# An encoder's MLP on one Trainium2 core: up-projection by seven block products, down-projection as a stage of its own

## The chip, the cores and the metric

The kernel runs on 1 core of one Trainium2 chip. Its time is the device time of that core in microseconds (us). Before the change the median of three runs is 2946.79 us (2944.85 to 2953.02).

The engines have their own instruction queues and run side by side: PE (TensorE, matrix products), DVE (VectorE), ACT (ScalarE), POOL (GpSimd) and SP (SyncE, which issues all DMAs here). SBUF is the on-chip memory of 128 partitions, PSUM the eight banks of 128 x 512 fp32 into which PE writes and adds up, DRAM the memory outside. "128x512" is partitions x elements of a tile.

## The reference, cut to what matters

Two layers (an attention mixer each, A and B) run over 1152 tokens: 1024 of a prompt and 8 samples of 16. What the change touches is the MLP that ends each layer, D = 1024, D_FF = 2816:

```python
def conv_ffn(h, prev, w_up, conv_w, conv_b, w_down):
    u = h @ w_up                                   # (1152, 1024) @ (1024, 5632)
    ue = concatenate([prev, u], axis=1)            # prev: zeros, or the sample's state
    y = conv_b
    for tap in range(3):
        y = y + conv_w[tap] * ue[:, tap:tap + T]   # causal, over positions
    a, g = jnp.split(y, 2, axis=-1)
    out = (jax.nn.gelu(g) * a) @ w_down            # (1152, 2816) @ (2816, 1024)
    return out, ue[:, T:]                          # the last rows are an output too

h = x * (1 + sc_f) + sh_f
f, conv_rows = conv_ffn(h, ...)
x = layer_norm(ALPHA * x + (1 + g_f) * f, ln_g, ln_b)
```

All is fp32. After layer 0 the K and V of layer 1 are projected from its output.

## The kernel before, in words

**Products in three passes.** PE works on fp32r. Each operand is held as a high part (a cast) and a low part (the operand minus its high part), made by `split` (L157 the cast, on ACT as a rule, L168 the subtraction, on POOL for weights, on DVE for activations). A product is low x high + high x low + high x high, three matmuls that add up in one PSUM bank. H, the input of a projection, stands in SBUF as `H[128, 2, 8, 1152]`: two parts, eight blocks of 128 rows of D, 1152 tokens.

**Order.** The program is written in Python as one sequence; a scheduler places the instructions on the engines' queues by a time estimate of its own, in keeping with all dependencies. On the chip every queue runs in order, and an instruction that waits holds what stands behind it.

**Stages.** `opening`, `attention(0)`, `out_proj(0)`, `ffn(0)`, `attention(1)` (which begins with the projections of K and V), `out_proj(1)`, `ffn(1)`. `out_proj` works token tile by token tile (128 tokens, in the order 8, 0, 1, ..., 7) and closes each with `norm_tail`: the residual, layer norm, transposes on PE, the affine of the next stage, and the split into H. It shares the buffers of `ln_region` in the SBUF tile `F`.

**ffn.** D_FF is cut into 22 pieces j of 128 columns, each with an `a` half (gg = 0) and a `g` half (gg = 1) of the up weights. `up(j, gg)` loads one weight block of 128 x 1024 (512 KB, `wload`: a ring of two load buffers `ws`, then the split into a ring of four slots `wh`/`wl`) and runs three blocks of 384 to 388 tokens (`up_block`; `mmT`, L287): 24 matmuls into one bank. A block reaches back two to four tokens, so that the convolution can be done from PSUM at once (`conv`): one ACT pass (L1011) and two to four DVE taps (L1014) that read the bank, POOL's addition of the samples' state (L1029). For gg = 1 the GELU (L1058, ACT), the product with `a` (L1060, POOL) and a split into `X` follow. The gated activations of two j's thus stay in SBUF.

`down(g)` takes the two j's of group g: for each of nine token tiles and two halves of 512 output columns six matmuls (L1085) into a bank, which DVE adds to `acc[128, 9216]` in SBUF (L1076). Up blocks and down blocks of neighbouring groups interleave on PE. The last group (`down_last`) goes tile by tile, with the residual and the gate already in `acc` (`pregate`: L1144 on POOL, L1145 on DVE) and the gate in the weights; each tile is closed by `norm_tail` (layer 0) or `norm_last` (layer 1).

**Background.** In layer 0's ffn the adaLN projections of later stages (`ada`, L206 the loads, L214 the matmuls; 64 loads of 512 KB) run as background work, a bit per `wload`. At its start stand `tables_b` and `skew(1)`, which write the bias table of mixer B to DRAM: the copy L1187, 6144 KB.

Of the kernel before, what the change touches and what calls it, by code (L numbers as in the profile page):

```python
# [16 lines left out]
NT = 9  # L17
# [77 lines left out]
class Trunk:  # L95
    def __init__(self, ctx, tc, I, O):
# [9 lines left out]
        self.x2p = ctx.enter_context(tc.tile_pool(name="x2p", bufs=1))  # L106
# [8 lines left out]
        self.X2 = mem.tile([128, 3840], F32R, name="X2")  # L115
# [25 lines left out]
        self.hmD = dr.tile([NT, 128, 1024], F32, name="hmD")  # L141
        self.gd = dr.tile([4, 9, D], F32, name="gd")
# [192 lines left out]
    def vproj(self, l, q, banks, tmp):  # L335
# [4 lines left out]
        for t in LV:  # L340
# [20 lines left out]
    def attention(self, l, wk):  # L361
# [5 lines left out]
        self.X1 = self.x1p.tile([128, 9216], F32R, name=f"x1att{l}", tag="x1")  # L367
# [15 lines left out]
        x2b = self.x2p.tile([128, 768], F32, name=f"x2att{l}", tag="x2b")  # L383
        rb = x2b[:, 0:512]
        sd = Arena(x2b, 512)
# [14 lines left out]
        L = sd.take(128)  # L400
        M = sa.take(128) if l == 0 else None
        ost = sa.ring(1, 512) if l == 0 else sd.ring(2, 64)
# [485 lines left out]
    def norm_tail(self, t, x, xdst, aff, save, tb, eh, er, xrr, hfr, el="v", va=()):  # L888
# [5 lines left out]
        if aff is not None:  # L894
# [51 lines left out]
    def out_proj(self, l, xsrc, xdst, aff):  # L946
# [13 lines left out]
        tb = Ring([4, 5, 6, 7])  # L960
        for t in (8, 0, 1, 2, 3, 4, 5, 6, 7):
# [13 lines left out]
            self.norm_tail(t, x, xdst, aff, False, tb, "a", "pv", Ring([self.xr]), Ring([self.hf]))  # L975


    def ffn(self, l, xsrc, xdst, affs):
        nc, I, O, H = self.nc, self.I, self.O, self.H
# [3 lines left out]
        acc = self.x1p.tile([128, 9216], F32, name=f"acc{l}", tag="x1")  # L983
        if l == 0:
            self.tables_b(acc)
            self.skew(1)
        st = acc[:, 0:704]
        nc.sync.dma_start(st, I["sc"][l])
        s4 = st.rearrange("p (c s q) -> p c s q", c=44, s=8)
        t1 = acc[:, 704 : 704 + 352].rearrange("p (c s) -> p c s", s=8)  # L990
# [9 lines left out]

        ub = Ring([0, 1, 2])
        db = Ring([3, 4, 5])
        tb = Ring([6, 7])
        x2 = Arena(self.X2)
        x2b = self.x2p.tile([128, 768], F32R, name=f"x2ffn{l}", tag="x2b")
        aring = Ring([(x2.take(384), x2.take(384)) for _ in range(5)] + [(x2b[:, 0:384], x2b[:, 384:768])])

        def conv(ps, cc, bi, y):
            w = lambda i: cw[:, cc, i : i + 1]
            off = 0 if bi == 0 else 4  # L1010
            nc.scalar.activation(y, ps[:, off : off + 384], AF.Identity, bias=w(3), scale=w(2))  # L1011

            def tap(o, u, i):
                nc.vector.scalar_tensor_tensor(o, u, w(i), o, op0=ALU.mult, op1=ALU.add)  # L1014

            if bi == 0:
                tap(y[:, 1:384], ps[:, 0:383], 1)
                tap(y[:, 2:384], ps[:, 0:382], 0)
            elif bi == 1:
                tap(y, ps[:, 3:387], 1)  # L1020
                tap(y, ps[:, 2:386], 0)
            else:
                tap(y[:, 0:256], ps[:, 3:259], 1)
                tap(y[:, 0:256], ps[:, 2:258], 0)
                ys = y[:, 256:384].rearrange("p (s q) -> p s q", q=16)
                us = ps[:, 260:388].rearrange("p (s q) -> p s q", q=16)
                tap(ys[:, :, 1:16], us[:, :, 0:15], 1)
                tap(ys[:, :, 2:16], us[:, :, 0:14], 0)
                nc.gpsimd.tensor_add(ys[:, :, 0:2], ys[:, :, 0:2], E4[:, cc])  # L1029

        UB = ((0, 384), (380, 388), (764, 388))

        acts = {}
        ya = {}

        def up(j, gg):
            w = self.wload(I["wup"][l, j + 22 * gg])
            for bi in range(3):
                up_block(w, j, gg, bi)

        def up_block(w, j, gg, bi):
            cc = j + 22 * gg
            s0, n = UB[bi]
            ps = self.bank(ub.next())
            self.mmT(w, ps, s0, n)
            if gg == 0:
                y = ya[bi] = self.ya.next()
            else:
                y = self.yg.next()
            conv(ps, cc, bi, y)  # L1050
            if bi == 2:
                uo = self.uo[gg].rearrange("p (j s r) -> p j s r", s=9, r=2)
                src = ps[:, 258:402].rearrange("p (s q) -> p s q", q=16)[:, :, 0:2]
                nc.scalar.copy(uo[:, j % 11], src)
                if j % 11 == 10:
                    nc.sync.dma_start(O["conv"][l, gg, j // 11], self.uo[gg])
            if gg == 1:
                nc.scalar.activation(y, y, AF.Gelu_apprx_tanh)  # L1058
                a = self.at.next()
                nc.gpsimd.tensor_mul(a, y, ya[bi])  # L1060
                h, lo = aring.next()
                self.split(a, h, lo, "a", "v")
                acts[(j, bi)] = (h, lo)

        def down(g):
            js = (2 * g, 2 * g + 1)
            w = [self.wload(I["wdn"][l, j]) for j in js]
# [379 lines left out]
```

## Time and profile before

| | |
|---|---|
| runs | 2944.85, 2946.79, 2953.02 us |
| profiled execution: span (the page gives its time as this) | 2951.8 us, granted clock 0.986 |
| PE busy | 2826.3 us, 96% |
| DVE busy | 1530.0 us, 52% |
| ACT busy | 1136.0 us, 38% |
| POOL busy | 893.7 us, 30% |
| DMA | 353.97 MB, mean 120 GB/s |
| ffn(0) | first up block at about 483 us, end among the K and V projections, about 1390 us |
| ffn(1) | first up block at 2091 us, last matmul at 2934.7 us |

A row of a group reads: line, engine, operation, output <- inputs, shapes, count | busy us, mean ns of one | idle us of the engine just before it, and who ended that idle time. A row of the timeline reads: start us, length us, engine, line, operation, tiles, count, and in brackets the idle time before it with its releaser. A row of the chain of waits has start, length and what it was. PEld is PE's loading of the stationary operand, which overlaps the matmuls.

### The profile page before, as it was taken

The numbers are of one execution on the slowest core, as the hardware profiler recorded it, in microseconds if no ns is written. First come the engines' busy times: TensorE is split into PE (matmuls) and PEld (weight loads), VectorE is DVE, ScalarE is ACT, GpSimd is POOL, SyncE is SP. The second block draws the span as 40 slices with busy tenths as digits, with TensorE's granted clock in tenths as the row PEclk, the third lists the DMA queues.
The fourth block names the chain that finished last, engine by engine and source line by source line (L and its number), as shares of the span: only waits on it lengthen the run. The fifth ranks groups of instructions, "written<-read, shape, count | busy, mean of one in ns | idle before, by whom it ended". The sixth has DMA issues, their size and how long they took to land.

```text
span 2951.8 us, 43469 instructions
## 1 busy us (share of the span) xinstructions
PE 2826.3 (96%) x16774; PEld 2534.2 (86%) x16774; DVE 1530.0 (52%) x3349; ACT 1136.0 (38%) x2352; POOL 893.7 (30%) x657
## 2 busy tenths in 40 slices
PE   7999899999999999998999999879999999999996
PEld 5888678898999988987998888758999999999995
DVE  4476776234444444469113677667624444444468
ACT  3476634322222222225435666642442222222224
POOL 2122524232232222254641111321432222222253
PEclk9999899999999999999999999999999999999999
DMA  8655455423222222124875457763311111111121
GB/s 295 203 174 154 140 158 184 140 89 100 90 85 76 88 81 100 54 79 152 292 244 173 133 149 203 188 189 117 126 50 37 43 44 46 39 41 43 37 84 76
DMA packets 177839, 353.97 MB, mean 120 GB/s; under 512 B 34816, under 2 KB 93904, under 8 KB 177632
## 3 DMA queue, kind: packets, MB, share of 16 engines
q1 hardware_dynamic: 177632, 351.19, 37.3%
q8 instruction: 132, 2.16, 0.3%
q14 instruction: 75, 0.61, 0.1%
HBM read 285.22 MB, written 75.35 MB: 122 GB/s over the span
## 4 chain that ended last, share of the span: by engine, by line
PE 79%; DMA 7%; DVE 5%; POOL 3%; ACT 2%; issue 2%; SPq 1%; DVEq 0%; POOLq 0%; ACTq 0%
PE PS L287 43%; PE PS L1085 16%; PE PS L299 9%; PE PS L584 2%; PE PS L562 2%; PE PS L214 2%; PE PS L534 1%; DMA F<-in_adaw_dram 1%; PE PS L537 1%; POOL wl L168 1%; DMA ws<-oN 1%; PE PS L703 1%; DMA F<-zd 1%; PE PS L902 1%; DVE acc L1145 1%
## 5 line engine op out<-in xcount | busy, mean ns | idle before, releaser
L287 PE MATMUL PS<-H,wh 128*128 128x388 f32 (+1 forms) x5376 | 1024.0, 338 | 0.0
L287 PEld LDWEIGHTS PS<-H,wh 128*128 128x128 f32 x5376 | 948.2, 188 | 10.4 <-issue 1.9
L1014 DVE SCALAR_TENSOR_TENSOR F<-PS,F 128x256 f32<-128x256 f32 (+2 forms) x704 | 352.8, 512 | 525.0 <-ACT F L1011 511.8
L168 POOL TENSOR_TENSOR wl<-ws,wh 128x1024 fp32r<-128x1024 f32 x166 | 404.5, 2442 | 725.6 <-ACT wh L157 711.3
L287 PE MATMUL PS<-H,wl 128*128 128x384 f32 (+1 forms) x2688 | 550.0, 342 | 10.9 <-POOL wl L168 9.4
L287 PEld LDWEIGHTS PS<-H,wl 128*128 128x128 f32 x2688 | 477.0, 188 | 33.8 <-POOL wl L168 12.9
L1011 ACT ACTIVATE F<-PS,F 128x384 f32<-128x384 f32 x264 | 177.5, 672 | 746.9 <-PE PS L287 745.7
L1085 PE MATMUL PS<-wh,X 128*128 128x512 f32 x1320 | 412.1, 394 | 10.3 <-DVE acc L1076 4.2
L1076 DVE TENSOR_TENSOR acc<-acc,PS 128x512 f32<-128x512 f32 x324 | 221.4, 686 | 262.8 <-PE PS L1085 262.2
L1060 POOL TENSOR_TENSOR F<-F 128x384 f32<-128x384 f32 x132 | 138.3, 1048 | 639.7 <-ACT F L1058 638.4
L1085 PEld LDWEIGHTS PS<-wh,X 128*128 128x128 f32 x1320 | 245.3, 188 | 62.9 <-issue 6.2
L157 ACT CAST wh<-ws 128x1024 fp32r<-128x1024 f32 x174 | 180.0, 1045 | 152.8 <-PE PS L1085 74.7
L1085 PE MATMUL PS<-wl,X 128*128 128x512 f32 x660 | 216.2, 392 | 0.0
L299 PE MATMUL PS<-wh,H 128*128 128x256 f32 (+1 forms) x936 | 173.3, 314 | 7.6 <-DVE H L168 4.1
L299 PEld LDWEIGHTS PS<-wh,H 128*128 128x128 f32 x936 | 136.7, 194 | 18.0 <-DVE H L168 4.7
L168 DVE TENSOR_TENSOR X<-F,X 128x384 fp32r<-128x384 f32 x110 | 101.0, 918 | 92.3 <-ACT X L157 91.9
L1085 PEld LDWEIGHTS PS<-wl,X 128*128 128x128 f32 x660 | 124.1, 188 | 28.0
L562 PE MATMUL PS<-C,F 128*128 128x128 f32 x720 | 115.0, 285 | 23.9 <-DVE wh L569 12.2
L622 POOL TENSOR_TENSOR F<-F,x2att 64x512 f32<-64x512 f32 x62 | 79.4, 1281 | 191.0 <-DVE F L598 159.3
L299 PE MATMUL PS<-x1att,H 128*128 128x512 f32 x504 | 130.1, 399 | 4.2 <-ACT x1att L157 3.1
L562 PEld LDWEIGHTS PS<-C,F 128*128 128x128 f32 x720 | 85.6, 145 | 42.5 <-DVE wh L569 15.1
L1058 ACT ACTIVATE F<-F 128x384 f32<-128x384 f32 x132 | 69.2, 524 | 135.6 <-DVE F L1014 127.4
(220 smaller groups left out, 3479.4 us busy)
## 6 DMA issues: line engine op xcount, KB each, us to landing
ws<-in_wup_dram SPq DMA_DIRECT2D x88, 512.0 KB
F<-in_adaw_dram SPq DMA_DIRECT2D x80, 512.0 KB
ws<-in_wdn_dram SPq DMA_DIRECT2D x44, 512.0 KB
ws<-in_adaw_dram SPq DMA_DIRECT2D x32, 512.0 KB
x1att<-kH SPq DMA_DIRECT2D x60, 256.0 KB
xd<-F SPq DMA_DIRECT2D x27, 512.0 KB
F<-xd SPq DMA_DIRECT2D x27, 512.0 KB
vH<-X SPq DMA_DIRECT2D x40, 256.0 KB
```

Source lines behind the costliest of these rows:

```text
L157: nc.scalar.copy(out, in_)
L168: self.eng(el).tensor_sub(lo, src, hi.bitcast(F32))
L287: self.nc.tensor.matmul(out[:, 0:n], w[a][:, k * 128 : k * 128 + 128], H[:, p, k, s0 : s0 + n], start=i == 0, stop=i == 23)
L299: self.nc.tensor.matmul(out[:, 0:n], H[:, p, j * kn + k, t0 : t0 + 128], w[a][:, k * n : k * n + n], start=i == 0, stop=i == 23,)
L562: nc.tensor.transpose(t[:, n * 128 : n * 128 + 128], p[:, (kt - k0) * 128 : (kt - k0) * 128 + 128], self.ident)
L622: self.eng("v" if last else "p").tensor_mul(on[r, q], on[r, q], rb[r, :])
L1011: nc.scalar.activation(y, ps[:, off : off + 384], AF.Identity, bias=w(3), scale=w(2))
L1014: nc.vector.scalar_tensor_tensor(o, u, w(i), o, op0=ALU.mult, op1=ALU.add)
L1058: nc.scalar.activation(y, y, AF.Gelu_apprx_tanh)
L1060: nc.gpsimd.tensor_mul(a, y, ya[bi])
L1076: nc.vector.tensor_add(row[:, n], row[:, n], ps)
L1085: nc.tensor.matmul(ps, ac[m][p][:, cs], w[m][q][:, n], start=i == 0, stop=i == 5)
```

## The change

The up-projection of 42 of the 44 pieces goes over to Strassen's scheme (in Winograd's form). The product for one j is seen as 2 x 2 blocks. The weights (both halves of one j, `a` and `g`, by the two halves of D) give a11, a12, a21, a22; H by the two halves of D and by the two 64-token halves of each token tile gives b11, b12, b21, b22. Seven block products replace eight:

- The weights' combinations S1 to S3 and a21' are made per j by POOL (four operations of 128x512), and each of the seven sub-weights is split (ACT cast, DVE subtraction).
- H's combinations T1 to T4 are made once per layer (`combine`, `first`): `out_proj` stores the affine output of each tile to DRAM (`hD`), `combine` loads it tile by tile through two buffers, POOL and DVE combine, ACT and DVE split. T1 takes the place of b12 in H, T2 and T3 stand in the tile that was `acc`, T4 in X2.
- A product is 12 matmuls on 320 columns (token tiles 0 to 4) and 12 on 256 (tiles 5 to 8). Products that share terms add up in the same banks; ACT copies and DVE additions read the partial sums out into rows `ua`, `ug` of SBUF (`evict`).
- The convolution reads these rows (`conv_row`): passes of 1152 on ACT, taps of 1024 on DVE, all from SBUF. GELU and product follow on the whole row, and the gated row goes to DRAM (`actD`).
- The first j of each layer (NPL = 1) is computed as before (`plain`), while the combinations are made.
- The ring of load buffers has four entries in this stage; the ada loads of layer 0 go through it as well.

The down-projection is a stage of its own (`down`). Three groups of three token tiles are computed one after the other, each over all 22 j's, in six banks: nothing is added up in SBUF any more. Per group and j the weights are loaded and split again, and 128x384 of the gated activations are read back and split. The gate, the residual and the norm follow per tile (`tail`). In layer 1's last group six j's are held back and run tile by tile (KEEP). `tables_b`, `skew(1)` and the loads of gates and norm rows stand at the start of `down`. The diff, cut to its core:

```diff
-LO = ((0, 1, 2, 8, 3, 4, 5, 6, 7), (0, 1, 2, 3, 4, 5, 8, 6, 7))
-UP = ({0: (0, 1), 2: (2,)}, {0: (0, 1), 3: (2,)})
-LV = (0, 1, 2, 8, 3, 4, 5, 6, 7)
+LV = ((0, 1, 2, 8, 3, 4, 5, 6, 7), (0, 1, 2, 6, 7, 8, 3, 4, 5))
+GR = ((0, 1, 2), (6, 7, 8), (3, 4, 5))
+NPL = 1
+BGU = 0.5
+KEEP = 6
...
+        self.hD = dr.tile([NT, 128, 1024], F32, name="hD")
+        self.actD = dr.tile([NFF, 128, TOK], F32, name="actD")
...
+            if hdst is not None:
+                nc.sync.dma_start(hdst[t].rearrange("p (c t) -> p c t", t=128), h3)
...
+        def gated(j, ya, yg):
+            nc.scalar.activation(yg, yg, AF.Gelu_apprx_tanh)
+            nc.gpsimd.tensor_mul(yg, yg, ya)
+            nc.sync.dma_start(self.actD[j], yg)
...
+        def combine():
+            ring = Ring([F[:, 1536:2560], F[:, 7548:8572]])
+            for t in (8, 0, 1, 2, 3, 4, 5, 6, 7):
+                s = ring.next()
+                nc.sync.dma_start(s, self.hD[t])
...
+                x1 = T1S[:, :, t, :]
+                nc.gpsimd.tensor_sub(x1, b12, b11)
+                nc.gpsimd.tensor_sub(b12, b22, b12)
+                nc.vector.tensor_sub(b22, b22, x1)
+                nc.vector.tensor_sub(b21, b21, b22)
+                c = slice(64 * t, 64 * t + 64)
+                for src, (hi, lo) in ((b22, T2), (b12, T3), (b21, T4)):
+                    self.split(src, hi[:, :, c], lo[:, :, c], "a", "v")
...
+        def spair(j):
+            sa, sg = self.ws.next(), self.ws.next()
+            nc.sync.dma_start(sa, I["wup"][l, j])
+            nc.sync.dma_start(sg, I["wup"][l, j + 22])
+            a11, a12, a21, a22 = sa[:, 0:512], sa[:, 512:1024], sg[:, 0:512], sg[:, 512:1024]
+            E = nc.gpsimd
+            E.tensor_add(S1, a21, a22)
+            E.tensor_sub(S2, S1, a11)
+            E.tensor_sub(S3, a11, a21)
+            E.tensor_sub(a21, a12, S2)
...
+            plan = (
+                (a11, 11, 0, True),
+                (S2, 2, 1, True),
+                (a12, 21, 0, False),
+                (S3, 3, 1, False),
+                (S1, 1, 2, True),
+                (a22, 4, 1, False),
+                (a21, 22, 2, False),
+            )
+            for i, (src, q, g, start) in enumerate(plan):
+                w = sub.next()
+                self.split(src, *w, "a", "v")
+                x = operand(q)
+                for n in range(2):
...
+                    for a, p in ((1, 0), (0, 1), (0, 0)):
+                        for k in range(4):
+                            nc.tensor.matmul(
...
+                    evict(i, ps, n)
+                self.step(BGU)
+                if i == 5:
+                    yg = ys.next()
+                    conv_row(ug, j, 1, yg)
+            ya = ys.next()
+            conv_row(ua, j, 0, ya)
+            gated(j, ya, yg)
+
+        for j in range(NPL):
+            plain(j)
+        self.ws = wide
+        if l == 0:
+            self.bg = [self.ada(g, 7, wide) for g in (3, 4, 5, 6)]
+        combine()
+        first()
+        for j in range(NPL, NFF):
+            spair(j)
+        self.drain()
+        self.ws = narrow
+        self.down(l, xsrc, xdst, affs)
...
+        def fetch(j, t0):
+            w = self.wload(I["wdn"][l, j])
+            s = raw.next()
+            nc.sync.dma_start(s, self.actD[j][:, t0 * 128 : t0 * 128 + 384])
+            a = acts.next()
+            self.split(s, *a, "a", "v")
+            return w, a
...
+        for gi, g in enumerate(GR):
+            keep = KEEP if l and gi == 2 else 0
+            for j in range(NFF - keep):
+                w, a = fetch(j, g[0])
+                for i in range(3):
+                    mm(j, w, a, i)
+            if gi == 0:
+                aff = affs()
+            kept = [(j, *fetch(j, g[0])) for j in range(NFF - keep, NFF)]
+            for i, t in enumerate(g):
+                for j, w, a in kept:
+                    mm(j, w, a, i)
+                tail(t, i)
```

More of the change, by code (lines that the diff above doesn't have):

```diff
@@ L999, in ffn @@
         g.tensor_mul(E4[:, :, :, 1], s4[:, :, :, 1], wb(0))
-        ub = Ring([0, 1, 2])
[L1002 to L1009, printed above, removed]
+        ys = Ring([F[:, o : o + 1152] for o in (10492, 6396, 7548)])
@@ L1041, in up_block @@
-        def up_block(w, j, gg, bi):
-            cc = j + 22 * gg
[L1043 to L1063, printed above, removed]
```

313 lines of the change are left out of this document (184 added, 129 removed).

## The prediction

> **What bounds the kernel now.** I read the page first (its totals and the chain that ended last), then windows of the two MLPs: length, busy time of PE, PE weight load, DVE, ACT and POOL, granted clock, DMA share, GB/s.
>
> ```profile
> span 2951.8 us, 43469 instructions
> PE 2826.3 (96%) x16774; PEld 2534.2 (86%) x16774; DVE 1530.0 (52%) x3349; ACT 1136.0 (38%) x2352; POOL 893.7 (30%) x657
> ...
> PE PS L287 43%; PE PS L1085 16%; PE PS L299 9%; PE PS L584 2%; PE PS L562 2%; PE PS L214 2%; PE PS L534 1%; DMA F<-in_adaw_dram 1%; PE PS L537 1%; POOL wl L168 1%; DMA ws<-oN 1%; PE PS L703 1%; DMA F<-zd 1%; PE PS L902 1%; DVE acc L1145 1%
> ```
>
> ```profile
> 505.00:1440.00 935.00, 918.14 (x5179) 829.89 (x5178) 422.73 (x759) 279.79 (x487) 300.63 (x219) 0.99 0.30 104
> 2106.00:2870.00 764.00, 763.67 (x4011) 718.49 (x4010) 330.00 (x554) 220.88 (x374) 229.19 (x169) 1.00 0.15 48
> 2870.00:2952.00 82.00, 56.80 (x276) 49.26 (x274) 70.14 (x148) 36.27 (x59) 31.96 (x18) 0.92 0.21 80
> 2343.00:2419.00 76.00, 76.00 (x400) 71.37 (x399) 32.85 (x57) 20.45 (x34) 21.12 (x16) 1.00 0.14 42
> ```
>
> The up-projection (L287, which also serves the K and Q projections) and the down-projection (L1085) carry 59% of the chain. PE has next to no gap in layer 1's MLP up to 2870, while DVE, ACT and POOL work less than half of it. So the price of a matmul is what counts, and work on the others costs nothing until PE has to wait for it.
>
> The paces come from rows that follow one another without a gap (start, length, what, count):
>
> ```profile
> 2345.27 1.43 PEld L287 LDWEIGHTS PS<-H,wl 128*128 128x128 f32 x8
> 2349.46 1.43 PEld L287 LDWEIGHTS PS<-H,wl 128*128 128x128 f32 x8
> 2353.70 1.42 PEld L287 LDWEIGHTS PS<-H,wl 128*128 128x128 f32 x8
> ...
> 1520.27 59.00 PE PS L299 x492
> 2343.84 39.79 PE PS L287 x226
> 2419.39 39.79 PE PS L287 x226
> ```
>
> One up block is 24 matmuls: 4.19 us at 384 columns, 4.24 at 388, so 176.7 ns each at 388. Three blocks are 12.67 us, both halves of one j 25.34. At 256 columns 492 matmuls took 59.00 us: 119.9 ns. A straight line through 256 and 388 gives 147.4 at 320. The last two rows are two j's apart: 75.55 less 4 x 12.67 leaves 24.87 for 108 matmuls of the down-projection, 4.14 us for 18. The profiled execution spans 2951.8 us, 5.0 above the median of the runs (2946.79) and inside their range; the sum is made against the span and 5.0 taken off at the end.
>
> **1. Seven products.** 42 of the 44 j's (one per layer stays plain) go from 144 matmuls to 7 x 24 = 168: 84 x 147.4 + 84 x 119.9 = 22.45 us against 25.34. That is 2.89 less, times 42: **-121.4**. Four products read H in runs of 64 columns; no row has a PE operand in such runs, so its price lies between nothing and the whole gain (none can come of it). I take nothing: in every row above the time follows the count of columns. Merging X2, the order of tiles in vproj and the moved buffers add no instruction: nothing.
>
> **2. What seven products ask of DVE and POOL.**
>
> ```profile
> L168 DVE TENSOR_TENSOR X<-F,X 128x384 fp32r<-128x384 f32 x110 | 101.0, 918 | 92.3 <-ACT X L157 91.9
> L1014 DVE SCALAR_TENSOR_TENSOR F<-PS,F 128x384 f32<-128x384 f32 x176 | 108.7, 617 | 92.9 <-ACT F L1011 87.3
> L1076 DVE TENSOR_TENSOR acc<-acc,PS 128x512 f32<-128x512 f32 x324 | 221.4, 686 | 262.8 <-PE PS L1085 262.2
> L350 DVE TENSOR_TENSOR X<-PS,X 128x256 fp32r<-128x256 f32 x40 | 17.0, 424 | 93.8 <-ACT X L349 93.8
> L1014 DVE SCALAR_TENSOR_TENSOR F<-PS,F 128x120 f32<-128x120 f32 x88 | 29.3, 333 | 0.0
> L622 POOL TENSOR_TENSOR F<-F,x2att 64x512 f32<-64x512 f32 x62 | 79.4, 1281 | 191.0 <-DVE F L598 159.3
> L168 POOL TENSOR_TENSOR wl<-ws,wh 128x1024 fp32r<-128x1024 f32 x166 | 404.5, 2442 | 725.6 <-ACT wh L157 711.3
> L1029 POOL TENSOR_TENSOR F<-F 128x16 f32<-128x16 f32 x88 | 21.6, 245 | 29.3 <-DVE F L1014 25.3 <-PE PS L1085 4.0
> ...
> 2366.76 0.56 DVE L168 TENSOR_TENSOR X<-F,X 128x384 fp32r<-128x384 f32 x1 [2.29 <-ACT X L157]
> 2007.33 1.23 DVE L974 SCALAR_TENSOR_TENSOR F<-F 128x1024 f32<-128x1024 f32 x1
> 2371.62 0.50 ACT L157 CAST X<-F 128x384 fp32r<-128x384 f32 x1
> ```
>
> DVE per j: seven low parts of 512 columns (0.70, between 0.56 at 384 and the 1.25 at 1024 of point 3) 4.9; five evictions from PSUM, each of 320, 192 and 64 columns (0.49, 0.36 and 0.23 on the line through 256 = 0.424 and 512 = 0.686), 5.4; four taps of 1024, now out of SBUF (1.23), and four small ones (0.33), 6.2. Together 16.5 of 22.45. POOL: four combinations of 512 (1.28), a product of 1152 (2.75 from 2.44 at 1024), two of 0.25: 8.4. ACT: seven casts (0.62, scaled from 0.50 at 384), five copies, three passes of 1152, about 11. SP: two loads and one store of 576 KB per j; the store waits for POOL's product and holds the next weight load behind it, which the four load buffers (a j and a half ahead) cover; without them a j would wait the 3.5 us that a load takes (point 3). Each fits. But where both inputs are in SBUF, the 384-column row averages 0.918 us though it takes 0.56 alone, and the tap that has one input in PSUM keeps to 0.617. Such operations wait for POOL. If they wait for all POOL does, DVE needs 16.5 + 8.4 = 24.9, 2.45 above PE: bounds 0 and +2.45 per j (a gain has no source, PE being at its columns). A collision costs 0.36 in that row with POOL busy 21 of 76 us; POOL's share becomes 8.4 of 22.45, but its operations half as long, so I take 0.3 for each of 15 operations: DVE 21.0 of 22.45. Close enough that its order costs PE something: +1.0 in layer 1, nothing in layer 0, where the background adds PE time (point 5). 21 x 1.0: **+21**.
>
> The Trainium skill (SBUF — State Buffer, "SBUF: two separate sides") speaks against the change here: a DVE operation with two SBUF inputs and a POOL operation that reads SBUF share a port pair as an exclusive lock, and whichever comes second is blocked for the whole instruction. The two DVE rows above agree (0.918 and 0.617). By the rule the port pair alone is held 11.1 + 8.4 = 19.5 us per j, which fits; with every POOL operation ahead of a DVE one it is the first rival below.
>
> **3. The combinations of H.** They go to DRAM tile by tile with out_proj's stores (18 stores in all, in a stage whose DMA is half idle: nothing), and come back through two buffers that the last tile's norm releases.
>
> ```profile
> 2091.20 1.47 PEld L287 LDWEIGHTS PS<-H,wl 128*128 128x128 f32 x8
> 2111.63 1.25 DVE L168 TENSOR_TENSOR H<-F,H 128x1024 fp32r<-128x1024 f32 x1 [3.31 <-ACT H L157]
> ...
> 345.49 0.36 SPq L172 DMA_DIRECT2D ws<-in_wo_dram  x1
> 348.96 1.05 ACT L157 CAST wh<-ws 128x1024 fp32r<-128x1024 f32 x1 [0.32 <-issue]
> 350.14 2.36 POOL L168 TENSOR_TENSOR wl<-ws,wh 128x1024 fp32r<-128x1024 f32 x1 [2.10 <-ACT wh L157]
> 352.53 0.34 SPq L172 DMA_DIRECT2D ws<-in_wo_dram  x1
> 356.41 1.04 ACT L157 CAST x1att<-ws 128x1024 fp32r<-128x1024 f32 x1 [0.22 <-DMA ws<-in_wo_dram]
> 358.61 2.37 POOL L168 TENSOR_TENSOR x1att<-ws,x1att 128x1024 fp32r<-128x1024 f32 x1
> ```
>
> The up stage starts at 2091.2; the last tile's H is split at 2112.9, and only then does the first load of nine start. A load lands about 3.5 us after issue (345.49 to 348.96); a tile then passes POOL twice (0.65), DVE twice and three splits in turn, about 3.6. Two buffers: 7.1 / 2 = 3.6 per tile; the ninth, then T1's own split, are done about 2150. Behind these tile by tile waits stand, on DVE and ACT, the plain j's evictions and the first sub-weights; nobody else waits for them. PE has the plain j (25.3), two transposes and the first and third product (6.4): covered to 2125. Between 13 (DVE's 2.1 us per tile alone) and 35 (1.4 more per tile for the evictions in between) I take 22 per layer, the chain of one tile being fixed by rows: **+44**. After a long wait the clock is granted late (0.66 in the row of point 4, 1.7 us lost in 5): three such waits, **+5**.
>
> **4. Down-projection.** The matmuls stay 1188 per layer. 324 additions of DVE into acc and POOL's 18 products go away: nothing, PE hid them. The weights are loaded three times: 88 more loads, casts and POOL subtractions, plus 132 reads of gated activations. The loop that sets the pace is one of two load buffers: issue, land, cast, subtract, issue again is 7.04 us in the rows above (345.49 to 352.53), 8.45 in the next (352.53 to 360.98): 3.5 to 4.2 per load against PE's 4.14. The read of 192 KB that goes ahead of each load adds at most 0.6 (at the 342 GB/s below). Bounds for 132 turns: 0, and (9.05 / 2 - 4.14) x 132 = +50; the undisturbed turn is the nearer, since nothing else loads here: **+7**. At the front of layer 0's down stage stands the 6 MB copy of the bias table that used to be at the start of its MLP:
>
> ```profile
> skb<-eb SPq DMA_DIRECT2D x1, 6144.0 KB
> ...
> 494.24 0.60 SPq L1187 DMA_DIRECT2D skb<-eb  x1
> 524.75 0.77 PE L214 MATMUL PS<-F,C 128*32 128x256 f32 x8 [2.21 <-DMA F<-in_adaw_dram]
> 515.00:520.00 5.00, 5.00 (x30) 5.00 (x30) 1.24 (x2) 1.34 (x3) 0.00 (x0) 1.00 0.97 342
> 525.00:530.00 5.00, 5.00 (x33) 4.05 (x29) 1.70 (x3) 1.55 (x3) 0.21 (x1) 0.66 0.68 238
> ```
>
> It fills the DMA queue some 25 us (0.97 of it) and what is issued behind it lands then (an ada load issued at 505.51 let PE go on at 524.75). In the changed order SP issues it in the last j, after the first down weight and ahead of the second. It ends about 8 us into the stage; second weight, cast and subtract make PE wait about 10, the four gate and norm rows (2 MB) behind it about 4 more: +14 (bounds 3 and 25); layer 1 has only the rows: +3. **+17.** Banks: each of four group changes waits for DVE's six gate products, about 2: **+8**; the end of layer 0, with three tails in one buffer, **+3**. Layer 1 holds back six j's for its last three tiles; if no lead has built up that is 16 lost, which I leave to the range.
>
> **5. What goes.** The old last group: PE idle 935 - 918 = 17 in layer 0's window, of which about 11 in the tiles of the end and the table's 2.2, and 25.2 after 2870, of which 17.2 lie behind the last matmul:
>
> ```profile
> 2934.31 0.40 PE L1085 MATMUL PS<-wh,x2ffn 128*128 128x512 f32 x1
> 799.66 4.30 PE PS L1085 x18
> 960.30 4.31 PE PS L1085 x18
> ```
>
> 11 + 8 = **-19**. The new end is gate, sum and norm of one tile, as now: **-1.5**. The last two rows (four j's, 160.64 against 151.1 in layer 1) show the ada background: 2.4 us of PE per j in layer 0, unchanged.
>
> Sum: -121.4 + 21 + 44 + 5 + 7 + 17 + 8 + 3 - 19 - 1.5 = -36.9; 2914.9 in the profile, **2910** for the median, 1.2% faster.
>
> **Rivals.**
> (a) DVE becomes the bound. Its two-input operations and POOL's take turns, PSUM evictions queue behind a blocked tap, PE waits for the bank. Full turns are 24.9; with 1.1 for the ACT pass that stands ahead of the copy of the first product DVE waits for (1152 columns, by the cast's row, less what overlaps) 26 per j, and in layer 0 26.7 (ada's additions): (26 - 23.45) x 21 + (26.7 - 24.85) x 21 = 92 more, 3002. It ends slower from 1.1 us per j above my 23.45 and 24.85. For it: the 0.918 row. Against it: 5.4 of DVE's work reads PSUM and collides with nothing. 0.20.
> (b) The covers hold: 22.45 per j, combinations 12 per layer, front 6, load loop 0, banks and ends 6: -121.4 + 24 + 2 + 6 + 6 - 19 - 1.5 = -104, 2843. For it: DVE at 73% without collisions. 0.22.
> (c) The load loop bounds the down stage: 4.5 per j (+50 in place of +7), and so no lead at the end (+16): 2969. For it: the 8.45 us turn. Against it: that turn held a load of another stage. 0.10.
> (d) My sum: 0.48.
>
> **Numbers.** 2910 is (d)'s. The range 2835 to 2990 leaves out somewhat over half of (a) and a third of (b), and holds (c); (d)'s own is 2880 to 2936. 0.3% (8.8 us) is about what a measurement of this kernel can tell from no change. Faster: (d), (b) and the mildest 0.02 of (a), 0.72; same: 0.05 of (a) and (c); slower: the rest of both, 0.23.
>
> **What would show it.** Starts of one j's first product 22.5 to 24 apart in layer 1 (right) or above 25.3 (a). PE's idle by releaser: DVE evictions of L1142 or splits of L171 for (a); between the plain j and the second product a wait of 15 to 30 us for DVE's xa, per layer. In the down stage 4.14 per j of 18 matmuls, with POOL's wl as releaser if (c). DMA above 0.9 around layer 0's change of stage with PE idle there. POOL's and DVE's mean lengths above 1.28 and 0.70 show the collisions. Wrong altogether if matmuls with 64-column runs are slower than 147 and 120 ns.

## The result, and the profile after

The changed kernel is slower: 2971.15 us median against 2949.9 beside it on the same chip, ratio 1.0065 (95% interval 1.0045 to 1.0085). The prediction said 2910, 1.2% faster. The profiled execution spans 2962.6 us, 10.8 more than the one of before. In what follows kernels that ran on other chips are compared by their ratio to the kernel before on the same chip; 0.1% is 3 us.

From the page after (the totals, then two of the slice rows, TensorE's busy share and its granted clock in tenths of 40 slices of 74 us, and the engines of the chain that ended last):

```profile
span 2962.6 us, 47567 instructions
PE 2743.6 (93%) x17782; PEld 2432.2 (82%) x17782; DVE 1894.1 (64%) x3702; ACT 1298.4 (44%) x2625; POOL 1138.2 (38%) x765
...
PE   7999899799999969999998999889889999998987
PEclk9999899899999989999999999999989999999999
...
PE 67%; DMA 8%; DVE 5%; issue 3%; ACT 2%; POOL 2%; SPq 1%; POOLq 0%; ACTq 0%; DVEq 0%
```

TensorE is busy 83 us less than before, and the span has grown: the matmuls did become fewer, and TensorE waits more. The dips of PE in the 8th and in the 29th and 30th slice are where each layer's MLP begins, the one in the 15th is the front of layer 0's new down stage, those in the 37th and 39th lie in layer 1's.

Windows of the same profile (length, busy time of PE, PE weight load, DVE, ACT, POOL, then granted clock, DMA share, GB/s): layer 0's down stage, layer 1's start of the MLP, 400 us of its products, and its down stage.

```profile
1060.00:1382.00 322.00, 291.58 (x1247) 231.14 (x1247) 175.62 (x187) 121.57 (x180) 184.05 (x76) 0.96 0.61 201
2095.00:2165.00 70.00, 43.82 (x227) 41.78 (x226) 46.51 (x83) 31.74 (x68) 33.31 (x33) 0.78 0.40 137
2190.00:2590.00 400.00, 400.00 (x3004) 400.00 (x3004) 317.99 (x540) 171.33 (x305) 162.32 (x126) 1.00 0.23 73
2628.00:2948.00 320.00, 285.21 (x1191) 227.30 (x1189) 188.29 (x183) 119.04 (x163) 172.45 (x71) 0.94 0.53 172
```

The third row is what the change was about: no gap on TensorE, VectorE busy 318 of 400 us. The time goes in the other three. What TensorE waited for there (who, for whom, us in total, times, longest), first layer 1's start, then its down stage, then layer 0's:

```profile
PE PS L1180 <- ACT H L160: 11.9, 1, 11.9
PE PS L290 <- ACT F L1032: 6.5, 1, 6.5
PE PS L1180 <- ACT xa L160: 5.8, 1, 5.8
...
PE PS L1246 <- DVE F L1260: 26.8, 2, 13.6
PE PS L1246 <- ACT H L160: 5.7, 1, 5.7
...
PE PS L1246 <- ACT wh L160: 23.8, 2, 14.8
PE PS L1246 <- POOL wl L171: 4.8, 4, 1.8
```

By stage, from the first matmul of one to the first of the next (layer 0's up stage to its last matmul, so that the 14.8 us wait behind it is counted with the down stage):

| stage | its matmuls without a gap | measured | lost |
|---|---|---|---|
| layer 1, up (a plain j, 21 j's of products, two transposes) | 25.3 + 470 + 1.6 = 497 | 532.6 (2095.5 to 2628.1) | 36: 26 idle, the rest late clock (0.78 in the second window) |
| layer 1, down | 66 x 4.2 = 277 | 319 (to 2947.4) | 42: 34 idle, the rest clock (0.94) |
| layer 0, up | 25.3 + 21 x 24.91 + 1.6 = 550 | 580 (480.8 to 1061.1) | 30: 26 idle |
| layer 0, down | 277 | 321 (to 1382.2) | 44: 30 idle |
| after the last matmul | | 15.2 (17.1 before) | -2 |

### The profile page after: what moved, and what is told of

Read it like the earlier page. It is cut to its first block, busy times and chain, and to the rows that moved or that the text cites. A ratio compares the mean times of both kernels' runs of the same rounds, so it can differ in the third digit from the quotient of the medians.

```text
span 2962.6 us, 47567 instructions
## 1 busy us (share of the span) xinstructions
PE 2743.6 (93%) x17782; PEld 2432.2 (82%) x17782; DVE 1894.1 (64%) x3702; ACT 1298.4 (44%) x2625; POOL 1138.2 (38%) x765
## 4 chain that ended last, share of the span: by engine, by line
PE 67%; DMA 8%; DVE 5%; issue 3%; ACT 2%; POOL 2%; SPq 1%; POOLq 0%; ACTq 0%; DVEq 0%
PE PS L1180 30%; PE PS L1246 13%; PE PS L302 9%; PE PS L290 8%; DMA ws<-in_wdn_dram 3%; PE PS L564 1%; PE PS L586 1%; PE PS L217 1%; DVE xa L171 1%; DMA F<-actD 1%; PE PS L536 1%; POOL H L171 1%; PE PS L539 1%; POOL wl L171 1%; PE PS L904 1%
## 5 line engine op out<-in xcount | busy, mean ns | idle before, releaser
L171 POOL TENSOR_TENSOR wl<-ws,wh 128x1024 fp32r<-128x1024 f32 x136 | 336.5, 2481 | 384.8 <-ACT wh L160 357.0
L1180 PE MATMUL PS<-H,wh 128*128 128x256 f32 (+1 forms) x2688 | 414.3, 297 | 0.0
L171 DVE TENSOR_TENSOR xa<-F,xa 128x384 fp32r<-128x384 f32 (+1 forms) x168 | 271.6, 1628 | 208.2 <-ACT xa L160 196.7
L1246 PE MATMUL PS<-wh,xa 128*128 128x512 f32 x1128 | 362.7, 400 | 39.1 <-ACT wh L160 23.8
L1180 PEld LDWEIGHTS PS<-H,wh 128*128 128x128 f32 x2688 | 379.3, 191 | 0.0
L1246 PEld LDWEIGHTS PS<-wh,xa 128*128 128x128 f32 x1128 | 214.2, 190 | 93.0 <-ACT wh L160 24.6
L1019 DVE SCALAR_TENSOR_TENSOR F<-F 128x1024 f32<-128x1024 f32 x336 | 264.8, 826 | 35.7 <-ACT F L1058 35.4
L1180 PE MATMUL PS<-H,wl 128*128 128x320 f32 (+1 forms) x1344 | 244.0, 301 | 27.6 <-ACT H L160 25.0
L290 PE MATMUL PS<-H,wh 128*128 128x384 f32 (+1 forms) x1344 | 262.2, 340 | 0.0
L171 DVE TENSOR_TENSOR wl<-F,wh 128x512 fp32r<-128x512 f32 x202 | 201.4, 1004 | 58.1 <-ACT wh L160 57.8
L290 PEld LDWEIGHTS PS<-H,wh 128*128 128x128 f32 x1344 | 236.9, 191 | 1.4 <-issue 1.0
L1180 PEld LDWEIGHTS PS<-H,wl 128*128 128x128 f32 x1344 | 200.4, 192 | 43.5 <-ACT H L160 25.7
L1246 PE MATMUL PS<-wl,xa 128*128 128x512 f32 x564 | 225.5, 400 | 5.0 <-POOL wl L171 4.8
L1246 PE MATMUL PS<-H,xa 128*128 128x512 f32 x684 | 167.1, 405 | 20.5 <-DVE F L1260 13.2
L1246 PEld LDWEIGHTS PS<-H,xa 128*128 128x128 f32 x684 | 132.2, 194 | 54.2 <-issue 13.6
```

Of the source, the lines that this page charges most:

```text
L171: self.eng(el).tensor_sub(lo, src, hi.bitcast(F32))
L290: self.nc.tensor.matmul(out[:, 0:n], w[a][:, k * 128 : k * 128 + 128], H[:, p, k, s0 : s0 + n], start=i == 0, stop=i == 23)
L1019: nc.vector.scalar_tensor_tensor(o, u, cw[:, cc, i : i + 1], o, op0=ALU.mult, op1=ALU.add)
L1180: nc.tensor.matmul(ps[:, 0:m], w[a][:, k * 128 : k * 128 + 128], x(p, k, n), start=start and c == 0, stop=c == 11, skip_group_check=True,)
L1246: nc.tensor.matmul(ps, a[p][:, i * 128 : i * 128 + 128], w[q][:, hf * 512 : hf * 512 + 512], start=j == 0 and c == 0, stop=j == NFF - 1 an ...
```

## The experiments

**The down stage alone.** All j's plain, the products and their combinations left out. (The four load buffers and layer 0's background then start ahead of the first j, and the background's rate is set so that it does as much per j as beside the products; these lines are left out below.)

```diff
-NPL = 1
+NPL = 22
...
-        combine()
-        first()
```

> All 22 j's of each layer as plain j's, the combinations of H left out (no seven-product j uses them), the new down stage as it is: the down stage alone, without the seven products. Theory A (the products are worth 42 x 2.96 = 124 us, the 52 us of idle TensorE at their start and some 13 of late clock behind it belong to them, and the down stage loses the rest by itself): 2971 + 124 - 65 = 3030 (3010 to 3045), with TensorE's idle in the down stage still 24 us in layer 0 and 34 in layer 1. Rival B (the seven products are what costs: their load on VectorE and GpSimd spills into the down stage): at or below 2971, and the down stage without its waits.

Measured: 3008.2 us, ratio 1.0191 (1.0168 to 1.0213). Theory B falls: the down stage costs 1.9% by itself, and the seven products win back 1.3%, some 37 us. It is 22 under theory A's number. TensorE idles 26 us in layer 1's down stage in place of 34, and 15 in layer 0's in place of 30, together 23 less. The two waits that shrank most:

```profile
PE PS L1246 <- DVE F L1260: 7.5, 2, 5.4
...
PE PS L1246 <- ACT wh L160: 5.5, 2, 3.8
```

In layer 1 (the first row) the wait for the gate products is 7.5 in place of 26.8, in layer 0 the front costs 5.5 in place of 23.8; other waits grew. So these two aren't fixed costs of the stage. For the front a cause is at hand: the scheduler (the "planner" of the expectations) issued the table's copy at 512.7 here, early in the up stage. For the gate products it isn't: their order in the queue is the one described next.

**The change of group in layer 1.** The changed kernel, from the end of the first group of three tiles to the start of the second, start and length first, DVE, POOL and PE rows:

```profile
2732.88 2.34 POOL L171 TENSOR_TENSOR H<-ws,H 128x1024 fp32r<-128x1024 f32 x1
2733.25 2.39 DVE L171 TENSOR_TENSOR xa<-F,xa 128x384 fp32r<-128x384 f32 x1 [4.64 <-ACT xa L160]
...
2741.00 2.34 POOL L171 TENSOR_TENSOR H<-ws,H 128x1024 fp32r<-128x1024 f32 x1 [1.14 <-ACT H L160]
2741.37 2.39 DVE L171 TENSOR_TENSOR xa<-F,xa 128x384 fp32r<-128x384 f32 x1 [1.09 <-ACT xa L160]
2743.68 1.27 DVE L1260 TENSOR_TENSOR F<-PS,F 128x512 f32<-128x512 f32 x2
2744.51 0.76 PE L1246 MATMUL PS<-wh,xa 128*128 128x512 f32 x1 [13.63 <-DVE F L1260]
```

TensorE ended the group at 2730.9. The gate products (L1260) that free its banks start at 2743.68, because low parts of the next group's activations (L171) stand ahead of them in VectorE's queue: eleven in the order that was built. Each waits for a load, and then for GpSimd's operation beside it; three were still to come when TensorE ended the group. The order alone doesn't make the wait: in layer 0, and in the kernel with plain j's alone, eleven stand there too, but most or all of them were through when the group ended (in layer 0 the last ended at 1180.9, with the group's last matmuls), and the waits for the gate products are 1.6 and 7.5 us in all. What set how far the loads had come by then wasn't taken apart. Two edits test this: put them behind the gate products, or take them off VectorE.

```diff
             for j in range(NFF - keep):
-                w, a = fetch(j, g[0])
+                with ExitStack() as es:
+                    if gi and 2 <= j < 14:
+                        es.enter_context(self.tc.issue_after(self.lastgate.ins))
+                    w, a = fetch(j, g[0])
```

> In the down stage's second and third group the low parts of the activations from the third j on stand behind the gate products of the group before in VectorE's queue; before, eleven of them stood ahead. Nothing else is changed. Theory A (in layer 1 the gate products stand behind low parts whose loads haven't come, 13.6 and 13.2 us of idle TensorE): both waits fall to 1 to 4 us, clock 3 us: 2971 - 25 = 2946 (2938 to 2955). Rival B (the load loop of two buffers is too slow for TensorE, 4.2 us a j, and the change of group is only where it shows): 2962 and more, with the same idle time now in waits for GpSimd's low parts of the weights.

```diff
-            self.split(s, *a, "a", "v")
+            self.split(s, *a, "a", "p")
             return w, a
```

> In the down stage the low parts of the activations (384 columns, one per j) are made by GpSimd in place of VectorE; VectorE then has only the tails. Theory A (planner's order: gate products stand in VectorE's queue behind low parts whose data haven't landed; moving these below the gates only put them behind the tail's norm): no low part is left on VectorE, so both kinds of wait go: of 26.8 us in layer 1 under 5 are left, clock 3 us: 2971 - 25 = 2946. Rival B (two load buffers bound the stage; GpSimd's part of the turn grows from 2.4 to 3.3): TensorE waits for GpSimd's low parts instead, 4.4 us or more per j, 2980 and more. Against VectorE: its 2.1 us mean for these low parts should show as 0.9 on GpSimd, so that the long time was a wait for GpSimd and not work.

Measured: the order alone 2966.8, ratio 1.0040 (1.0022 to 1.0058), which the changed kernel's interval overlaps; GpSimd for the low parts 2934.1, ratio 0.9936 (0.9919 to 0.9953), 38 us better than the changed kernel (33 of them in layer 1's down stage) and already faster than before. TensorE's waits in layer 1's down stage, the order first:

```profile
PE PS L1246 <- DVE C L874: 10.1, 1, 10.1
PE PS L1246 <- DVE C L878: 3.0, 1, 3.0
```

```profile
PE PS L1246 <- POOL H L171: 2.9, 2, 1.7
PE PS L1246 <- ACT H L160: 2.3, 1, 2.3
L171 POOL TENSOR_TENSOR xa<-F,xa 128x384 fp32r<-128x384 f32 x61 | 67.5, 1113 | 0.3 <-ACT xa L160 0.2
```

With the new order the waits for the gate products are gone, and 13.1 us of new ones stand in their place: now the low parts wait behind the tail's statistics (L874, L878). So half of 26.8 was won in layer 1, whose stage takes 305.8 us in place of 319.3, while layer 0's became 8 us longer, with more waits for weights. The reason was right; the cure moved half of the wait to another place. With the low parts on GpSimd both go, the stage takes 286.0 us in place of 319.3. That is 9 over 277, 4.33 per j, with the same two load buffers and a longer turn through GpSimd: rival B of both expectations, the load loop as what costs the 42, is out. The last row is the low part on GpSimd, 1.11 us on average; on VectorE the same operation averaged 2.09 (below).

**The table's copy in layer 0.** Start of layer 0's down stage in the changed kernel, the copy's issue, the matmul that waits, and two windows (DMA share and GB/s at the end):

```profile
1037.83 0.38 SPq L175 DMA_DIRECT2D ws<-in_wdn_dram  x1
1045.83 0.61 SPq L1317 DMA_DIRECT2D skb<-eb  x1
1076.13 1.22 PE L1246 MATMUL PS<-wh,xa 128*128 128x512 f32 x2 [14.83 <-ACT wh L160]
...
1050.00:1060.00 10.00, 10.00 (x78) 10.00 (x78) 3.25 (x12) 2.38 (x3) 2.40 (x1) 1.00 1.00 306
1060.00:1070.00 10.00, 1.30 (x11) 1.10 (x10) 3.68 (x7) 1.48 (x4) 0.22 (x1) 0.79 1.00 297
```

```diff
-            self.tables_b(F[:, 1152:3200])
-            self.skew(1)
...
         for j in range(NPL, NFF):
+            if l == 0 and j == 3:
+                self.tables_b(...)
+            if l == 0 and 4 <= j < 20:
+                nc.sync.dma_start(...)  # one head of the copy
             spair(j)
```

> The 6 MB copy of the bias table taken out of the front of layer 0's down stage: its table is made at j = 3 of layer 0, and the copy goes head by head, 384 KB each, one per j from j = 4. Theory A (the 14.8 and 9.0 us of idle TensorE at that front are the copy in the DMA queue): 24 less and 3 of clock, 2944 (2936 to 2952), no wait over 4 us there. Rival B (the waits are the two load buffers starting from nothing): 2960 and more, with the waits where they were. Against the place of the copies: in layer 0's up stage a weight may come late, seen as idle TensorE of over 1 us per j there.

> As the one before with the bias table's copy spread over layer 0's j's, but the table is made in a free buffer of the gated activations' ring (the first one wrote it over the convolution's weights, so what it left is only a time). Theory A: as there, idle TensorE at the front of layer 0's down stage 10 in place of 24 us, the ratio to before 1.0029 in place of 1.0065: 2958 to 2963. If the wrong weights had any hand in the time, 2966 and more.

The first wrote its table over the convolution's weights, so it computes something else, and only its time is of use. Measured: ratios 1.0029 (1.0018 to 1.0041) and 1.0009 (0.9998 to 1.0020) against 1.0065, 11 and 17 us. Waits at that front in the second one, for its whole down stage of layer 0:

```profile
PE PS L1250 <- ACT wh L160: 6.8, 2, 5.6
PE PS L1250 <- POOL wl L171: 6.5, 7, 1.8
```

6.8 in place of 23.8, so 17 of the 24 us were the copy, 13.6 in the first wait (14.8) and 3.4 in the second (9.0 at 1103.9). Theory A holds for that. Sixteen copies of 384 KB cost some 2 us in the up stage (582 in place of 580). The 5.6 left in the second wait aren't the copy's. The traces point to the rows of gates and norm: SP issues them from 1085.65 to 1090.9 in the changed kernel, the DMA share is 1.0 from 1090 to 1100 and the wait ends at 1103.9; in the kernel without the copy the gates' rows go out from 1089.8, the share is 1.03 from 1095 to 1100, the wait ends at 1104.9. No run moved these rows, so that is not shown.

**The combinations of H.** First more plain j's ahead, then the same with the second load buffer moved:

```diff
-NPL = 1
+NPL = 3
```

> Three plain j's ahead of the products in place of one, per layer. Theory A (the 26 us of idle TensorE per layer between the first plain j and the products are the chain of combinations, 55 us long, which two more plain j's of 25.3 us cover): 4 x 2.96 = 12 us more of columns, 52 of idle and some 13 of late clock less, 2918 (2908 to 2930). Rival B (the combinations stand behind the plain j's own evictions on VectorE and ScalarE, so that more plain j's push them back): half of it or less, 2945 and more, with TensorE still idle over 12 us per layer ahead of the second product.

```diff
-NPL = 1
+NPL = 3
...
-            ring = Ring([F[:, 1536:2560], F[:, 7548:8572]])
+            ring = Ring([F[:, 1536:2560], F[:, 8700:9724]])
```

> The changed kernel with three plain j's again, and nothing else but the second of the two combination buffers moved from the one that the plain j's activations also use to a spare weight buffer. Theory A (that shared buffer put four of the nine loads behind the store of the third plain j's activations in SP's queue): TensorE's 20 to 23 us of idle per layer ahead of the second product become 3 or less, and some 6 us per layer of late clock and 3 of other waits go with it: 2997 - 55 = 2942; below the changed kernel if the cover is worth its 12 us of columns. Theory B (two buffers don't suffice, or the planner strings the loads out for another reason): 2975 and more, with the idle time where it was.

The first was a clear miss: 2996.9, ratio 1.0148 (1.0126 to 1.0170), slower than with one plain j, and TensorE still waits ahead of the products in layer 1. SP's queue shows why (L1083 loads H for the combinations, L1067 stores a plain j's activations):

```profile
PE PS L1180 <- ACT xa L160: 19.6, 1, 19.6
...
2187.84 0.32 SPq L1083 DMA_DIRECT2D F<-hD  x1
2198.31 0.32 SPq L1067 DMA_DIRECT2D actD<-F  x1
2217.39 0.33 SPq L1067 DMA_DIRECT2D actD<-F  x1
2220.17 0.33 SPq L1083 DMA_DIRECT2D F<-hD  x1
```

No load is issued between 2187.84 and 2220.17: the buffer at column 7548 also holds activations of the plain j's, and the loads that need it stand behind the third one's store. With that one buffer moved the ratio is 1.0039 (1.0025 to 1.0053), 32 us less. The 19.6 us wait is gone; the longest that is left at this place:

```profile
PE PS L290 <- DVE F L1019: 5.2, 1, 5.2
```

That is theory A for the shared buffer, and layer 1's up stage takes 514 us to its last matmul in place of 532.6, but 2966.1 is 24 above the theory's number. 14 of it is layer 0's down stage, where TensorE idles 43.8 us against 30.2 in the changed kernel, 33.6 of them for casts of weights at its front, where this kernel issues the table's copy (1073.0, the stage's first matmul 1072.3). Then with one plain j, four buffers in place of two, and the work without seven of the nine loads:

```diff
-            ring = Ring([F[:, 1536:2560], F[:, 7548:8572]])
+            ring = Ring([F[:, o : o + 1024] for o in (1536, 7548, 8700, 11644)])
```

> The combinations of H come back through four load buffers in place of two (the two spare weight buffers, not used until the second j of products). Theory A (the chain of loads with two buffers, a turn of 8 to 11 us for two tiles, is what TensorE waits for): nine tiles at the 3 us of their work, the chain 52 us long becomes 35, idle TensorE per layer 26 becomes 10 and the clock loses 3 less: 2971 - 38 = 2933. Rival B (SP's and VectorE's order: loads behind the store of the first j's activations and the additions behind the evictions): idle at 20 or more per layer, 2960 and more.

```diff
-                nc.sync.dma_start(s, self.hD[t])
+                if t in (8, 0):
+                    nc.sync.dma_start(s, self.hD[t])
```

> On the changed kernel: of the nine loads of H for the combinations only the first two are made; the other seven tiles are combined from what the two buffers hold, so the work on GpSimd, VectorE and ScalarE stays, the loads go, and the output isn't the reference's. Theory A (the loads are the chain): idle TensorE ahead of the second and third products 26 us per layer becomes 8 or less, 2971 - 44 = 2927. Theory B (four buffers brought only 5 us per layer: the chain is the work, in the places that the planner gave it in the queues, behind the plain j's conv, gelu and GpSimd's product): 20 or more idle per layer, 2955 and more.

Measured: 1.0045 (1.0029 to 1.0062) and 0.9981 (0.9970 to 0.9991). Layer 1's up stage takes 527.4 and 522.9 us against 532.6, and TensorE's idle time ahead of the products is 22 and 19 us against 26; in layer 0 it is 21 and 15 against 26. So the loads are the smaller part, 18 of 52 us. The rest is put down to the work on GpSimd, VectorE and ScalarE in the places where it stands, which no run varied by itself, and neither theory gives the numbers. More cover takes most of it away (under "Together").

**VectorE's load.**

```diff
             tap(y[:, 0:1024], u[:, 0:1024], 0)
+            nc.vector.tensor_tensor(y[:, 0:1024], y[:, 0:1024], y[:, 0:1024], op=ALU.max)
```

> On the changed kernel: each j of products gets two more VectorE operations of two SBUF inputs and 1024 columns (the maximum of the gated activations' inputs with themselves, which changes nothing), 1.23 us alone and 1.28 as the taps beside them: VectorE's 19.4 us per j become 21.9, against TensorE's 22.38. Theory A (VectorE's load is no price until it exceeds TensorE's): a j stays at 22.4 to 22.9 in layer 1, 2971 to 2990. Theory B (the prediction's step 2: close to TensorE's time its order costs 1 us per j and more, and the collisions with GpSimd grow): 24 us or more per j, 3035 and more.

Measured: 2964.5, ratio 1.0036 (1.0022 to 1.0051), no slower than the changed kernel. 400 us of layer 1's products:

```profile
2200.00:2600.00 400.00, 400.00 (x3007) 400.00 (x3007) 351.82 (x577) 173.55 (x306) 163.00 (x127) 1.00 0.21 72
L1061 DVE TENSOR_TENSOR F<-F 128x1024 f32<-128x1024 f32 x37 | 45.0, 1217 | 0.0
```

VectorE is busy 352 of 400 us, the added operations take 1.22 us each, and TensorE has no gap. Theory A: up to 88% its load cost nothing in this loop. A kernel with more work and the same pace reads 0.3% lower here than the changed one did on its chip. So a difference of that size between ratios from different chips isn't resolved: the new order's 0.25% and the four buffers' 0.20% rest on the waits in the traces, not on the times.

**Together.** The three edits with one plain j, then with two and three load buffers that no plain j uses:

> The three edits together: the table's copy spread, GpSimd for the low parts of the activations, four buffers for the combinations. Theory A: the gains lie at different places and add up: 2971 - 10 - 25 - 38 = 2898, below the kernel before. Rival B (each wait that goes leaves the next one, in the same two load buffers): 2935 and more.

```diff
-NPL = 1
+NPL = 2
...
+            ring = Ring([F[:, o : o + 1024] for o in (1536, 8700, 11644)])
```

> The three edits together as before, but two plain j's ahead of the products, and the combinations' loads in three buffers of which none is a buffer of a plain j's activations (with three plain j's one of the two was). Theory A (what went wrong with three plain j's was that shared buffer): the combinations hide, idle TensorE ahead of the products 5 us or less per layer in place of 20 and 22, 3 us of columns more per layer: 2914 - 30 = 2884. Theory B (the planner strings the combinations out between the plain j's evictions whatever the buffers): idle stays at 15 or more per layer, 2914 and more.

Measured: 2914.4, ratio 0.9865 (0.9847 to 0.9884), and 2879.7, ratio 0.9750 (0.9719 to 0.9782): the second is 2.5% faster than the kernel before. The single gains (1.29, 0.56 and 0.20%) sum to 2.05%, the three together gave 2.00%: they lie at different places, as theory A of the first said, though the combinations' part was smaller than expected. The last step changes two things, the cover and the buffers, and they weren't tried apart. Start of layer 1's MLP, its products and its down stage in the last kernel, and its waits at that start:

```profile
2065.00:2135.00 70.00, 61.44 (x347) 60.59 (x346) 51.36 (x96) 31.70 (x71) 29.86 (x31) 0.95 0.41 137
2135.00:2535.00 400.00, 400.00 (x3003) 400.00 (x3003) 318.52 (x540) 174.28 (x309) 167.62 (x131) 1.00 0.24 77
2577.00:2861.00 284.00, 279.04 (x1190) 222.23 (x1188) 78.99 (x123) 119.52 (x163) 234.73 (x131) 1.00 0.59 193
...
PE PS L1180 <- ACT xa L160: 3.8, 1, 3.8
PE PS L290 <- POOL F L1088: 3.3, 1, 3.3
```

With a third of 1.5 that is 8.6 us of idle in place of 26 (in layer 0 14 in place of 26), more than the 5 that theory A allowed, and the granted clock is 0.95 there in place of 0.78; layer 1's down stage runs at 283 us.

## Why the prediction was wrong

It had the sign wrong, and the step that failed is the down stage: +35 was charged, and it lost +86. The combinations cost 17 more than charged, and 21 for VectorE's load, which cost nothing, hid part of both. By its own steps, in us, from the profiles:

| step | predicted | measured | what it was |
|---|---|---|---|
| 1, columns of the seven products | -121.4 | -122 | layer 1 2.96 per j, layer 0 27.75 - 24.91 = 2.84 |
| 2, load on VectorE and GpSimd | +21 | 0 | 22.38 per j |
| 3, combinations, with the clock behind them | +49 | +66 | 36 and 30 |
| 4, down stage | +35 | +86 | 42 and 44 |
| 5, last group and end | -20.5 | -19 (not seen again) and -2 | |
| sum | -37 | +9 | the profiles say +10.8 |

The 86 are counted over 4.2 per j, the pace of the changed kernel's down matmuls; over the prediction's 4.14 they would be 94 and the sum +17. The prediction took that pace as unchanged.

**Step 1** holds. Two rows of one product of the changed kernel, 200 us apart, and a product that reads H in runs of 64 columns, up to the next one (X is T4, read in one run):

```profile
2205.79 0.76 PE L1180 MATMUL PS<-xa,wl 128*128 128x320 f32 x4
2407.22 0.76 PE L1180 MATMUL PS<-xa,wl 128*128 128x320 f32 x4
...
2305.50 1.33 PE L1180 MATMUL PS<-H,wh 128*128 128x320 f32 x8
2306.67 0.64 PE L1180 MATMUL PS<-H,wl 128*128 128x256 f32 x4
2307.14 1.12 PE L1180 MATMUL PS<-H,wh 128*128 128x256 f32 x8
2308.10 0.75 PE L1180 MATMUL PS<-X,wl 128*128 128x320 f32 x4
```

201.43 us are nine j's of 22.38. From start to start, 8 matmuls of 320 columns take 1.17 us and 8 of 256 take 0.96: 146 and 120 ns, the predicted paces, and that with H read in runs of 64 columns.

**Step 2** had the work right and its price wrong. VectorE's busy time is 318 / 400 x 22.38 = 17.8 us per j, against 16.5 without collisions and 21.0 with the 15 of 0.3 that I charged. The groups of layer 1's products (2190 to 2610) show where they are:

```profile
L171 DVE TENSOR_TENSOR wl<-F,wh 128x512 fp32r<-128x512 f32 x92 | 88.2, 959 | 12.5 <-ACT wh L160 12.5
L171 DVE TENSOR_TENSOR wl<-ws,wh 128x512 fp32r<-128x512 f32 x39 | 52.4, 1344 | 3.9 <-ACT wh L160 3.8
L1019 DVE SCALAR_TENSOR_TENSOR F<-F 128x1024 f32<-128x1024 f32 x77 | 98.3, 1277 | 0.1
```

Low parts take 0.96 and 1.34 where 0.70 was their length alone, the taps 1.28, so the row that I took the collision from was a fair one for the low parts and not for the rest. What failed here is the next sentence: "close enough that its order costs PE something: +1.0". Nothing in a row gave that number, and the run with more load shows none. Rival (a)'s 26 per j was never near.

**Step 3** named the right wait at the right place. 22 per layer was 26 on TensorE; the clock behind it, charged 5 for three waits, was some 10 in layer 1 alone, since after these waits it runs at 0.78 over 70 us. The chain ran to 2164 and not 2150.

**Step 4** is where the sign was lost. "Each of four group changes waits for DVE's six gate products, about 2: +8" counted the products and not what stands ahead of them in VectorE's queue; the two waits of layer 1 were 13.6 and 13.2, those of layer 0 1.6 in all. The order that was built shows the eleven low parts, so the risk could have been read before the run, though not its size. The front of layer 0 had its mechanism named and its size wrong: 10 predicted for the copy and 4 for the rows behind it, 14.8 and 9.0 measured, of which 17 went with the copy. The load loop, +7 for both layers, was somewhat low: layer 1's stage without the waits for VectorE is 9 over its matmuls, 5 of it idle.

**The rivals.** (c) gave 2969 and the time was 2971, by chance: its load loop of 4.5 per j didn't bound the stage, as the 4.33 with the low parts on GpSimd and the same two buffers showed. (b), the covers hold, was right for the pace of the products and wrong everywhere else. Waits for VectorE, in the up stage the mark of (a), came in the down stage, where VectorE was busy 188 of 320 us: it was not load but what stood ahead in its queue. The rest between the table's sum and the profiles, 2 us over or 6 under by the base of step 4, isn't resolved; profiles of unchanged stages differ by more (layer 0's MLP starts between 480.8 and 489.9 in them).

## What to carry to other kernels

Price a change that adds a stage by what stands ahead of each releasing instruction in its engine's queue and by when its data come, not by that instruction's length: here six products of 0.68 us held TensorE for 13, with VectorE busy 59% of the stage. Work fetched ahead is best kept off the engine that frees the banks at the seam: moving the 66 low parts of each layer from VectorE to GpSimd was worth 38 us, changing their order alone 7 at most. A buffer shared between two chains orders them (32 us with three plain j's), and a large copy is better spread over a stage whose DMA queue has room (17 us): by such moves the same change became 2.5% faster than the kernel before.

## What was unexpected in the hardware

VectorE's low part of 384 columns, 0.56 us alone, took 2.09 on average in the down stage, and 2.4 next to GpSimd's 2.34 us operation; the pairs shown from 2733 and 2741 end within 0.5 us of each other. The same operation on GpSimd took 1.11.

```profile
L171 DVE TENSOR_TENSOR xa<-F,xa 128x384 fp32r<-128x384 f32 x53 | 110.4, 2093 | 92.2 <-ACT xa L160 80.9 <-DMA ws<-in_wdn_dram 11.2
```

The Trainium skill (SBUF — State Buffer, "SBUF: two separate sides") calls the pair of ports that such operations share an exclusive lock, held for the whole instruction. The trace agrees here. Over the loop of the products TensorE noticed nothing of it: VectorE is busy 17.8 us and GpSimd 9.1 per 22.38, and 2.4 us more of such operations lengthened VectorE's busy time by 1.9 and the loop not at all.
